# Attention evaluated in tile pairs: low parts of the odd tiles on VectorE, later padded values, value products in one step, query means and logarithms apart

## The chip, the cores and the metric

One core of one Trainium2 chip. The metric is the device time of one execution in microseconds (us), given as the median of three runs.

## The reference

A decoder trunk of two layers on an input of 1024 tokens by 1024 channels in float32. Layer 0 mixes tokens by a short gated convolution, layer 1 by sliding-window attention with sixteen query heads, four key/value heads and a window of 128; each mixer is followed by a SwiGLU feed-forward part. The change lies in layer 1's mixer, of which this is the core:

```
q = rmsnorm(q, q_gain); k = rmsnorm(k, k_gain)        # per head, 64 wide
scores = einsum('bnqkgd,bnskd->bnkgqs', qb, kw) * scale
scores = scores + alibi;  scores = where(mask, scores, -inf)
p = softmax(concat([scores, sink_col], -1))[..., :-1]
out = einsum('bnkgqs,bnskd->bnqkgd', p, vw)
out = out.reshape(bsz, s, N_Q_HEADS * HEAD_DIM) @ w_o
```

## The kernel before, in words

**Split operands.** All large products are made in float32 precision from two rounded operands: a high part (a copy rounded by ScalarE or VectorE) and a low part (what the rounding left out, by a subtraction). A product is three matmuls: high by high, high by low, low by high.

**Tiles, pairs and units.** The sixteen heads lie in eight tiles of 128 channels (two heads each), numbered 0 to 7; tiles 2p and 2p+1 are pair p. The attention takes one tile and one block of 128 queries at a time, a unit `(tile, block)`. `units` (L2408) lists 64 of them, numbered n here: pair p has units 16p to 16p+15, block by block, the even tile at even n and the odd tile at odd n. So unit 1 is tile 1's first block, unit 17 that of tile 3, unit 33 of tile 5, unit 49 of tile 7.

**Steps and their order.** All engines execute their instructions in the order in which the program issues them, and this order is written by hand (`tc.manual_schedule`, L2547). `step` (L2426) issues one step of a software pipeline that has eight lead-in steps before unit 0; step n works on unit n and some before it. The string `ORDER` (L59) says what a step issues, a letter at a time:

- `S`: scores of unit n on TensorE (four matmuls, L2245 and L2246, into the one bank P0). `M`: VectorE adds the distance bias and takes the minima (L2260), which frees P0. `E`: ScalarE's exponentials of unit n-1 (L2280).
- `T`: TensorE turns unit n-2 (L2288) into bank P1 (odd tile) or P3 (even tile); `H` and `L`: its high part by ScalarE (L2323) and low part by VectorE (L2329). Whichever of P1 and P3 isn't being turned into is `pos["free"]`, and statistics and rows (below) use it.
- `V`: the value products of a pair of units (L2343). Sub-block 0 is issued at even n for the units n-4 and n-3, sub-block 1 at odd n for n-5 and n-4. Each is up to four matmuls of 256 columns into one bank. `O` (odd n) and `o` (even n): ScalarE copies half of the result out (L2358), VectorE adds the other half (L2360), and the bank is free.
- `D`: what is due of the softmax division: sums widened by GpSimd (L1803), turned by TensorE (L1808), multiplied in by VectorE (L2388).
- `P`: a piece of other TensorE work. Through unit 39 it is the projection of the next pairs' queries (`work_of_pairs`, L2517; matmuls L2004), three pieces a step with 21 matmuls in four steps; from unit 40 on the first half of the output projection (L171, L175).
- `k` and `K`: what has been planned for the half step and for the end of the step. `plan(d, f)` (L2413) puts f d steps ahead.

**A tile's queries.** When the projection of a tile is finished, `keep_q` (L2137) plans its normalisation over the next steps: squares by ScalarE (L2146); at 2.5 steps, in a `k`, statistics by TensorE (sixteen matmuls with two columns, L1678), the mean by VectorE (L1685) and the logarithm by ScalarE (L1697); at 3, in the `K`, ScalarE's exponential (L1702) and a Newton step in VectorE's four small instructions (L1704 to L1711); the result is widened by GpSimd (L1803), turned by TensorE (L1808) and multiplied in by VectorE (L1813); then, per half of the tokens and per head, a high part by ScalarE (L2176) and a low part by GpSimd (L2181, function `part_lo`). `later` shifts the whole plan by so many steps. With it go GpSimd's low parts of the weights (`split_granule`, L1948, after VectorE's high part L1947), which are loaded by the sync engine's queue (L1941), and streamed operands on the same queue (L2507).

**Padded values.** The value products need copies of the values with 64 of the 128 rows zeroed. `load_padded` (L2310) has GpSimd zero the room on its first call (L2307, L2308) and then issues two DMAs of 128 KB (L2316) on the sync engine's queue.

Of the kernel before, what the change touches and what calls it, by code (L numbers as in the profile page):

```python
# [12 lines left out]
AF = mybir.ActivationFunctionType  # L13
# [42 lines left out]
KEYS_AS_PAIR = 4  # L56
STREAMED = (5, 2, 3, 4)

ORDER = "SPTMEoDkPHLVOPK"  # L59


EARLY = 4
# [25 lines left out]
def trunk_kernel(ctx: ExitStack, tc: tile.TileContext, xT, small, w_in, w_out, w_q, w_v, w_o, w_gu, w_dn, out):  # L88
# [1571 lines left out]
    def attention_layer():  # L1660
# [36 lines left out]
            act.activation(y, m, AF.Ln)  # L1697
            return y

        def head_guess(y, inv):  # L1700

            act.activation(y, y, AF.Exp, scale=-0.5)  # L1702
            t = slot("hr_t", (P, NB, 2), bufs=2)
            dve.tensor_tensor(t, y, y, ALU.mult)  # L1704
            if inv is not None:
                dve.tensor_tensor(y, y, inv.unsqueeze(1).to_broadcast([P, NB, 2]), ALU.mult)
            return t
# [429 lines left out]
        def keep_q(i, raw_of, side=None, later=0, steps=False):  # L2137

            t = {}

            def squares(h):
                if "raw" not in t:
                    t["raw"] = raw_of()
                    wide = slot("X2" if i else q_tag(i, 1)) if side is None else side
                    t["side"] = [wide[:, h * 512 : h * 512 + 512] for h in (0, 1)]
                act.activation(t["side"][h], t["raw"][:, h * 512 : h * 512 + 512], AF.Square)  # L2146

            def stats_of(b0=0, n=NB):
                if "st" not in t:
                    t["st"] = bank(pos["free"])  # L2150
                for b in range(b0, b0 + n, 2):
                    head_stats(t["st"], t["side"][b // 4][:, b % 4 * P : (b % 4 + 2) * P], b, 2)

            def mean():
                t["m"] = head_mean(t["st"])
                t["y"] = head_log(t["m"])

            def guess():
                t["t"] = head_guess(t["y"], cst[:, C_INVS + 2 * i : C_INVS + 2 * i + 2])

            def newton():
                head_newton(t["y"], t["t"], t["m"])


            def halves(e):
                rows = [slice(0, HD), slice(HD, P)]
                return rows[e], rows[1 - e]

            def raw_half(h, rows):
                return t["raw"][rows, h * 512 : h * 512 + 512].rearrange("p (s q) -> p s q", q=SUB)  # L2170

            def part_hi(h, e):
                rows, _ = halves(e)
                if e == 0:
                    Q.setdefault(i, []).append(slot(q_tag(i, h), (P, 8, 2, SUB), F32R))
                act.copy(Q[i][h][rows, :, e, :], raw_half(h, rows))  # L2176

            def part_lo(h, e, eng=pool):
                rows, rest = halves(e)
                q = Q[i][h]  # L2180
                eng.tensor_tensor(q[rest, :, e, :], raw_half(h, rows), plain(q)[rows, :, e, :], ALU.subtract)  # L2181

            rows_of = lambda h: scale_rows(t["raw"], t["side"][h], h, bank(pos["free"]))
            wide_of = lambda h: spread(pool, t["side"][h], t["y"][:, 4 * h : 4 * h + 4, :])

            if steps:
                shared = lambda h: spread(act, t["side"][h], t["y"][:, 4 * h : 4 * h + 4, :])
                return SimpleNamespace(
                    squares1=lambda: squares(1),
                    squares0=lambda: squares(0),  # L2190
                    stats=stats_of,
                    mean=mean,
                    guess=guess,
                    newton=newton,
                    wide0=lambda: shared(0),
                    wide1=lambda: shared(1),
                    rows0=lambda: rows_of(0),
                    rows1=lambda: rows_of(1),
                    hi0=lambda: part_hi(0, 0),
                    hi1=lambda: part_hi(0, 1),  # L2200
                    hi2=lambda: part_hi(1, 0),
                    hi3=lambda: part_hi(1, 1),
                    lo0=lambda: part_lo(0, 0),
                    lo1=lambda: part_lo(0, 1, dve),
                    lo2=lambda: part_lo(1, 0),
                    lo3=lambda: part_lo(1, 1),
                )
            first, rows = 1, (4.5, 5.5)
            for d, fs in (
                (first, [lambda: squares(0)]),  # L2210
                (first + 0.5, [lambda: squares(1)]),
                (1.5 + first, [stats_of, mean]),
                (2 + first, [guess, newton]),
                (rows[0] - 1.5, [lambda: wide_of(0)]),
                (rows[0] - 0.5, [lambda: wide_of(1)]),
                (rows[0], [lambda: rows_of(0)]),
                (rows[0] + 0.5, [lambda: part_hi(0, 0)]),
                (rows[1], [lambda: rows_of(1), lambda: part_lo(0, 0)]),
                (rows[1] + 0.5, [lambda: part_hi(0, 1)]),
                (rows[1] + 1, [lambda: part_lo(0, 1)]),  # L2220
                (rows[1] + 1.5, [lambda: part_hi(1, 0)]),
                (rows[1] + 2, [lambda: part_lo(1, 0)]),
                (rows[1] + 2.5, [lambda: part_hi(1, 1)]),
                (rows[1] + 3, [lambda: part_lo(1, 1)]),
            ):
                for f in fs:
                    plan(d + later, f)
# [80 lines left out]
                pool.memset(plain(padded[p][1])[0:SUB], 0.0)  # L2308

        def load_padded(p, q):  # L2310
            if p not in padded:
                pad_rooms(p)
            for sub in (0, 1):
                rows = slice(sub * SUB, (sub + 1) * SUB)
                src = plain(v[q])[rows, :, p].rearrange("p b l d -> p b (l d)")
                nc.sync.dma_start(plain(padded[p][sub])[rows, 4 * q : 4 * q + 4], src)  # L2316
# [96 lines left out]
        def plan(d, f):  # L2413

            agenda.setdefault(pos["step"] + d, []).append(f)
# [10 lines left out]
        def step(work, full=True):  # L2426


            n = pos["n"]
            pos["n"] += full  # L2430
            at = lambda d, f: f(*units[n - d]) if full and 0 <= n - d < NU else None

            def value(d, sub):
                if full and 0 <= n - d < NU and (n - d) % 2 == 0:
                    i, b = units[n - d]
                    values(i // 2, b, sub)

            def rest(d, step_):
                if full and 0 <= n - d < NU and (n - d) % 2 == 0:
                    keep_o(*units[n - d], step_)  # L2440

            pos["piece"] = 0

            def piece():
                next(work, None)
                pos["piece"] += 1

            calls = {
                "S": lambda: at(0, scores),
                "T": lambda: at(2, turn),  # L2450
                "V": lambda: [value(4, 0), value(5, 1)],
                "O": lambda: rest(5, 0),
                "o": lambda: rest(6, 1),
                "M": lambda: at(0, maxima),
                "E": lambda: at(1, exponents),
                "D": lambda: [f() for f in due.pop(n, [])] if full else None,
                "H": lambda: at(2, turn_hi),
                "L": lambda: at(2, turn_lo),
                "P": piece,
                "k": planned_early,  # L2460
                "K": planned,
            }
            for c in ORDER:
                calls[c]()
# [52 lines left out]
        def work_of_pairs():  # L2517
            n = 0
            for j in range(n_first, len(seq)):
# [4 lines left out]
                for p in range(NK // 2):  # L2524
# [3 lines left out]
                    for i in range(3):  # L2528
                        next(steps)
                        n += 1  # L2530
                        if i == 2 and streamed:
                            after_use(used["n"])
                            used["n"] += 1
                        if i == 2 and p == NK // 2 - 1:
                            finish(u, k, soon)
                            if k == 1:
                                keep_q(2 * u, lambda u=u: raw_of_even(u))
                            if k == 4:
                                raw, side = raw_of_odd(u)
                                keep_q(2 * u + 1, lambda raw=raw: raw, side, later=2)  # L2540
                        if n % 7 in (2, 4, 5, 0):
                            yield
# [4 lines left out]
        with tc.manual_schedule(engines={E.PE, E.Activation, E.DVE, E.Pool, E.SP}):  # L2547
# [4 lines left out]
            for d, g, e in ((12, 0, 1), (28, 1, 0), (34, 1, 1)):  # L2552
                for i, dd in enumerate((0, 0.5, 1.5, 3.5)):
                    plan(d + dd, lambda g=g, e=e, i=i: it["part"](g, e, i))
            for d, p, q in ((1, 0, 0), (3, 0, 1), (18, 1, 0), (19, 1, 1), (38, 2, 0), (45, 2, 1), (52, 3, 0), (53, 3, 1)):
                plan(d, lambda p=p, q=q: load_padded(p, q))
            keep_q(1, lambda: rooms["odd"], later=0)
            work = work_of_pairs()
# [167 lines left out]
```

## Time and profile before

| what | value |
|---|---|
| median of 3 runs (lowest, highest) | 1961.82 us (1961.06, 1962.26) |
| the profiled execution, its time | 1957.65 us |
| its span, first to last instruction | 1955.8 us |
| TensorE busy, whole span | 1923.0 us (98%) |
| VectorE, ScalarE, GpSimd busy | 67%, 45%, 16% |
| TensorE's mean granted clock | 0.991 of full speed |

The profile's page shows the busy share of each engine over the span in 40 equal slices of 49 us, and the granted clock below them. The attention's pipeline fills slices 22 to 26 (about 1036 to 1276 us). A row of the time line is: start, length, engine, line, operation, what it writes and reads, how many instructions are merged in it, and in brackets how long the engine sat idle before it and which instruction's end released it. "SPq" is the sync engine's queue.

### The profile page before, as it was taken

The numbers are of one execution on the slowest core, as the hardware profiler recorded it, in microseconds if no ns is written. First come the engines' busy times: TensorE is split into PE (matmuls) and PEld (weight loads), VectorE is DVE, ScalarE is ACT, GpSimd is POOL, SyncE is SP. The second block draws the span as 40 slices with busy tenths as digits, with TensorE's granted clock in tenths as the row PEclk, the third lists the DMA queues.
The fourth block names the chain that finished last, engine by engine and source line by source line (L and its number), as shares of the span: only waits on it lengthen the run. The fifth ranks groups of instructions, "written<-read, shape, count | busy, mean of one in ns | idle before, by whom it ended". The sixth has DMA issues, their size and how long they took to land. (4 is left out here: it accounts for less than half of the span.)

```text
span 1955.8 us, 25343 instructions
## 1 busy us (share of the span) xinstructions
PE 1923.0 (98%) x8989; PEld 1602.0 (82%) x8989; DVE 1316.0 (67%) x2293; ACT 886.8 (45%) x1753; POOL 310.6 (16%) x394
## 2 busy tenths in 40 slices
PE   9999999999999999999998889899999999999999
PEld 8888888888888888888987778788888888888887
DVE  8898867966556666556856676688765656565543
ACT  5543555533333334444555676555333333344441
POOL 0001221021111100100025465210111111100000
PEclk9999999999999999999998899999999999999999
DMA  8897594478887639975556651251674666468562
GB/s 318 255 240 168 126 249 144 130 256 232 233 239 212 173 122 349 310 215 177 212 217 214 190 179 35 89 185 55 231 194 143 195 188 180 125 234 281 196 231 100
DMA packets 160991, 382.53 MB, mean 196 GB/s; under 512 B 15840, under 2 KB 31328, under 8 KB 160864
## 3 DMA queue, kind: packets, MB, share of 16 engines
q1 hardware_dynamic: 125472, 271.55, 41.0%
q0 software_dynamic: 35248, 109.33, 22.9%
q8 instruction: 71, 1.16, 0.2%
q14 instruction: 56, 0.46, 0.1%
q10 hardware_dynamic: 144, 0.03, 0.0%
HBM read 304.04 MB, written 152.57 MB: 233 GB/s over the span
## 5 line engine op out<-in xcount | busy, mean ns | idle before, releaser
L1004 PE MATMUL acc<-XS,G 128*128 128x512 f32 x926 | 360.4, 389 | 0.0
L1007 PE MATMUL acc<-XS,G 128*128 128x512 f32 x926 | 360.3, 389 | 0.0
L1005 PE MATMUL acc<-XS,G 128*128 128x512 f32 x926 | 360.2, 389 | 0.0
L1004 PE MATMUL P<-A,G 128*128 128x512 f32 x550 | 214.1, 389 | 0.0
L1007 PE MATMUL P<-A,G 128*128 128x512 f32 x550 | 214.0, 389 | 0.0
L1005 PE MATMUL P<-A,G 128*128 128x512 f32 x550 | 214.0, 389 | 0.0
L1004 PEld LDWEIGHTS acc<-XS,G 128*128 128x128 f32 x926 | 173.8, 188 | 36.1
L1007 PEld LDWEIGHTS acc<-XS,G 128*128 128x128 f32 x926 | 173.8, 188 | 36.1
L1005 PEld LDWEIGHTS acc<-XS,G 128*128 128x128 f32 x926 | 173.8, 188 | 36.1
L1004 PE MATMUL acc<-A,G 128*128 128x512 f32 x442 | 172.1, 389 | 0.0
L1007 PE MATMUL acc<-A,G 128*128 128x512 f32 x442 | 172.0, 389 | 0.0
L1005 PE MATMUL acc<-A,G 128*128 128x512 f32 x442 | 171.9, 389 | 0.0
L938 DVE TENSOR_TENSOR G<-WL,G 128x512 fp32r<-128x512 f32 x168 | 115.0, 685 | 73.4 <-ACT G L937 73.4
L938 DVE TENSOR_TENSOR G<-WR,G 128x512 fp32r<-128x512 f32 (+1 forms) x216 | 144.2, 668 | 29.6 <-ACT G L937 29.6
L937 ACT CAST G<-WR 128x512 fp32r<-128x512 f32 (+1 forms) x216 | 130.5, 605 | 64.5 <-PE acc L1007 26.8
L937 ACT CAST G<-WH 128x512 fp32r<-128x512 f32 (+1 forms) x174 | 104.6, 601 | 84.4 <-PE acc L1007 40.8
L938 DVE TENSOR_TENSOR G<-WH,G 128x512 fp32r<-128x512 f32 (+1 forms) x174 | 115.5, 664 | 21.5 <-ACT G L937 21.3
L1339 ACT ACTIVATE G<-G 128x512 f32<-128x512 f32 x88 | 55.8, 634 | 159.2 <-DVE G L1436 153.1
L1004 PEld LDWEIGHTS P<-A,G 128*128 128x128 f32 x550 | 103.2, 188 | 21.4
L1005 PEld LDWEIGHTS P<-A,G 128*128 128x128 f32 x550 | 103.2, 188 | 21.4
L1007 PEld LDWEIGHTS P<-A,G 128*128 128x128 f32 x550 | 103.2, 188 | 21.4
L901 POOL DMA_DIRECT2D s<-s x68 | 60.1, 893 | 353.1 <-DMA s<-s 173.2
(440 smaller groups left out, 3793.3 us busy)
## 6 DMA issues: line engine op xcount, KB each, us to landing
G<-h SPq DMA_DIRECT2D x70, 512.0 KB, 4.8
s<-in_w_dn SPq DMA_DIRECT2D x32, 704.0 KB, 8.2
h<-X POOLq DMA_DIRECT2D x44, 512.0 KB, 4.9
s<-s POOLq DMA_DIRECT2D x32, 704.0 KB, 7.3
WR<-s SPq DMA_DIRECT2D x79, 256.0 KB, 4.1
WR<-in_w_gu SPq DMA_DIRECT2D x36, 512.0 KB, 5.4
WH<-in_w_gu SPq DMA_DIRECT2D x36, 512.0 KB, 4.4
XS<-q_ops SPq DMA_DIRECT2D x36, 512.0 KB, 5.4
```

What stands on the lines that cost most here:

```text
L901: nc.gpsimd.dma_start(dst[to], dst[of], accum_op=ALU.add)
L937: lambda: act.copy(out_hi, raw),
L938: lambda: lo_eng.tensor_tensor(out_lo, raw, plain(out_hi), ALU.subtract),
L1004: pe.matmul(ps, w[:, 0, c], x[:, 0, :], start=start and e == 0, stop=False, skip_group_check=True)
L1005: pe.matmul(ps, w[:, 0, c], x[:, 1, :], start=False, stop=False, skip_group_check=True)
L1007: pe.matmul(ps, w[:, 1, c], x[:, 0, :], start=False, stop=last, skip_group_check=True)
L1339: state["silu"] = act.activation(x, x, AF.Silu)
```

## The change

Five things, all in the attention's schedule:

- `ORDER` gets a letter `v`: both sub-blocks of the value products are issued at odd n for the units n-5 and n-4, sub-block 0 early in the step (after the first `P`), sub-block 1 where `V` stands. At even n there is none.
- The statistics' plan: the logarithm and exponential move to the end of the step that has the statistics, behind `H` and `O`; VectorE's small instructions and GpSimd's first widening move to the middle of the next step.
- The even tiles 2, 4 and 6 start their plan one step later (`later=1`), so that their statistics are issued at n = 7, 23 and 39 and no longer at 6, 22 and 38. The odd tiles keep their steps (12, 28 and 44).
- For odd tiles the low parts of the first half of the tokens (two subtractions a tile) go to VectorE.
- Zeroing the padded rooms is planned by itself, at steps 4, 17, 37 and 51 after the pipeline's begin (before: inside the loads, at 1, 18 and 52); the first pair's loads are at 7 and 9 (before: 1 and 3).

```
-ORDER = "SPTMEoDkPHLVOPK"
+ORDER = "SPvTMEoDkPHLVOPK"
...
+        def head_exp(y):
             act.activation(y, y, AF.Exp, scale=-0.5)
+
+        def head_guess(y, inv, exp=True):
+
+            if exp:
+                head_exp(y)
             t = slot("hr_t", (P, NB, 2), bufs=2)
...
+            def mean_only():
+                t["m"] = head_mean(t["st"])
+
+            def log():
+                t["y"] = head_log(t["m"])
+
             def mean():
-                t["m"] = head_mean(t["st"])
-                t["y"] = head_log(t["m"])
-
-            def guess():
-                t["t"] = head_guess(t["y"], cst[:, C_INVS + 2 * i : C_INVS + 2 * i + 2])
+                mean_only()
+                log()
+
+            def guess(exp=True):
+                t["t"] = head_guess(t["y"], cst[:, C_INVS + 2 * i : C_INVS + 2 * i + 2], exp)
...
+            low = dve if i % 2 else pool
             for d, fs in (
                 (first, [lambda: squares(0)]),
                 (first + 0.5, [lambda: squares(1)]),
-                (1.5 + first, [stats_of, mean]),
-                (2 + first, [guess, newton]),
-                (rows[0] - 1.5, [lambda: wide_of(0)]),
+                (1.5 + first, [stats_of, mean_only]),
+                (2 + first, [log, lambda: head_exp(t["y"])]),
+                (2.5 + first, [lambda: guess(False), newton, lambda: wide_of(0)]),
                 (rows[0] - 0.5, [lambda: wide_of(1)]),
                 (rows[0], [lambda: rows_of(0)]),
                 (rows[0] + 0.5, [lambda: part_hi(0, 0)]),
-                (rows[1], [lambda: rows_of(1), lambda: part_lo(0, 0)]),
+                (rows[1], [lambda: rows_of(1), lambda: part_lo(0, 0, low)]),
                 (rows[1] + 0.5, [lambda: part_hi(0, 1)]),
-                (rows[1] + 1, [lambda: part_lo(0, 1)]),
+                (rows[1] + 1, [lambda: part_lo(0, 1, low)]),
...
         def load_padded(p, q):
-            if p not in padded:
-                pad_rooms(p)
...
-                "V": lambda: [value(4, 0), value(5, 1)],
+                "v": lambda: value(5, 0),
+                "V": lambda: value(5, 1),
...
                             if k == 1:
-                                keep_q(2 * u, lambda u=u: raw_of_even(u))
+                                keep_q(2 * u, lambda u=u: raw_of_even(u), later=1)
...
-            for d, p, q in ((1, 0, 0), (3, 0, 1), (18, 1, 0), (19, 1, 1), (38, 2, 0), (45, 2, 1), (52, 3, 0), (53, 3, 1)):
+            for d, p in ((4, 0), (17, 1), (37, 2), (51, 3)):
+                plan(d, lambda p=p: pad_rooms(p))
+            for d, p, q in ((7, 0, 0), (9, 0, 1), (18, 1, 0), (19, 1, 1), (38, 2, 0), (45, 2, 1), (52, 3, 0), (53, 3, 1)):
                 plan(d, lambda p=p, q=q: load_padded(p, q))
```

More of the change, by code (lines that the diff above doesn't have):

```diff
@@ L1698, in head_log @@
             return y
-        def head_guess(y, inv):
+        def head_exp(y):
             act.activation(y, y, AF.Exp, scale=-0.5)
+        def head_guess(y, inv, exp=True):
+            if exp:
+                head_exp(y)
             t = slot("hr_t", (P, NB, 2), bufs=2)
```

## The prediction

> **What bounds the kernel now.** I read the page first, then the busy time by stage, then TensorE's groups in the attention with what ended their idle time, then the time line around the longest gaps. The page says that TensorE is the bound, and where it isn't whole:
>
> ```profile
> PE 1923.0 (98%) x8989; PEld 1602.0 (82%) x8989; DVE 1316.0 (67%) x2293; ACT 886.8 (45%) x1753; POOL 310.6 (16%) x394
> PEclk9999999999999999999998899999999999999999
> ```
>
> ```profile
> 1036.00:1190.00 154.00, 135.00 (x813) 117.98 (x812) 107.18 (x330) 102.23 (x316) 81.25 (x80) 0.90 0.54 171
> 1190.00:1276.00 86.00, 78.25 (x477) 65.10 (x477) 59.29 (x170) 54.28 (x174) 32.31 (x43) 1.00 0.21 69
> 1276.00:1955.00 679.00, 675.77 (x2994) 558.96 (x2994) 420.63 (x646) 263.18 (x446) 57.45 (x88) 1.00 0.57 182
> ```
>
> The columns are the stretch, its length, busy time of TensorE, its weight loads, VectorE, ScalarE and GpSimd, the granted clock, the DMA share. TensorE idles 32.8 us of the 1955.8 us span, and 19.0 + 7.75 of these lie in the attention. From 1276 us on it is busy 675.77 of 679.00: what the attention saves the end keeps. What the 26.75 us wait for:
>
> ```profile
> L2245 PE MATMUL P<-A,G 128*128 128x192 f32 (+2 forms) x128 | 32.7, 279 | 11.4 <-POOL G L2181 9.7 <-DVE mx L2260 1.8
> L1678 PE MATMUL P<-cst,X 128*128 128x2 f32 x80 | 10.7, 264 | 8.3 <-DVE G L2388 6.9 <-DVE X L2329 1.3
> L2343 PE MATMUL P<-G,A 128*128 128x256 f32 x58 | 15.1, 305 | 4.9 <-DVE XS L2360 2.9 <-ACT WH L143 1.8 <-ACT s L2280 0.3
> L2343 PE MATMUL P<-X,A 128*128 128x256 f32 x40 | 11.1, 307 | 1.3 <-ACT G L2280 0.7 <-ACT G L2323 0.4 <-DVE A L2360 0.2
> L2343 PE MATMUL P<-G,G 128*128 128x256 f32 x38 | 8.5, 287 | 0.4 <-DVE A L2360 0.4
> ```
>
> Scores wait 11.4 us, 9.7 of it for GpSimd's low parts; statistics 8.3; value products 4.9 + 1.3 + 0.4 = 6.6. Together 26.3, and each is one of the change's targets. Behind most long gaps TensorE also runs at half clock. These are the stretches of the attention in which the clock's row is 0.50:
>
> ```profile
> 1040.52:1047.35 6.83, 4.85 (x15) 4.10 (x16) 2.00 (x7) 1.05 (x6) 5.66 (x5) 0.50 0.11 38
> 1078.07:1081.48 3.41, 3.41 (x14) 3.12 (x14) 1.65 (x8) 2.05 (x8) 2.27 (x3) 0.50 1.03 305
> 1095.14:1098.55 3.41, 3.41 (x13) 2.86 (x12) 2.18 (x7) 0.63 (x2) 0.86 (x2) 0.50 0.00 0
> 1115.62:1119.03 3.41, 3.41 (x13) 3.02 (x14) 1.25 (x6) 1.57 (x7) 0.96 (x2) 0.50 0.00 2
> 1136.10:1142.92 6.82, 6.82 (x27) 6.04 (x27) 4.95 (x13) 2.89 (x12) 5.82 (x6) 0.50 0.49 145
> 1173.64:1180.47 6.83, 6.83 (x26) 6.04 (x26) 2.13 (x10) 2.47 (x9) 2.40 (x3) 0.50 0.01 4
> ```
>
> They hold 28.73 us of busy TensorE; at full clock that work takes half, so they cost 14.4 us. A single one costs 1.7. At most 26.75 + 14.4 = 41 us could go.
>
> **The change part by part.** Times are of the profiled execution (span 1955.8, its own time 1957.65); it lies 4.2 us below the median of 1961.82, and I take the saving from the median.
>
> *Unit 1's scores.*
>
> ```profile
> 1030.52 2.28 SPq L2316 DMA_DIRECT2D A<-A  x2
> 1033.55 0.56 SPq L1941 DMA_DIRECT2D WR<-in_w_q  x1
> ```
>
> ```profile
> 1039.19 0.43 DVE L1947 CAST WL<-WR 128x512 fp32r<-128x512 f32 x1 [3.33 <-DMA WR<-in_w_q]
> 1039.79 0.41 DVE L2260 CUSTOM_DVE_ANT_0 s<-P,cst 128x128 f32<-128x128 f32 x1
> 1041.19 2.60 POOL L2181 TENSOR_TENSOR G<-WH,G 64x512 fp32r<-64x512 f32 x2
> 1042.50 0.42 PE L2245 MATMUL P<-A,G 128*128 128x64 f32 x1 [3.67 <-POOL G L2181]
> ```
>
> ```profile
> L2181 DVE TENSOR_TENSOR G<-G,G x1: 777/777/777, 1024.5 to 1024.5; 64x512 fp32r<-64x512 f32 x1
> ```
>
> The padded loads hold the sync queue 2.28 us ahead of a weight load, for which VectorE then waits 3.33 us; GpSimd's low parts (1.3 us each) stand behind GpSimd's part of the same weights. Moved to steps 7 and 9, the padded loads let the weights go between 0 and 2.28 us earlier; an operand load between them still waits for TensorE, so I take 1.3. The low part on VectorE costs 0.78 us and stands before unit 0's minima, whose end (1040.20) frees P0. So unit 1's scores start at 1040.20 + 0.78 - 1.3 = 1039.7 instead of 1042.50: 2.8 us. With 0.9 us of idle left the half clock behind it goes too: 4.85 / 2 = 2.4. Sum **5.2**; bounds 1.5 (weights no earlier, half clock stays) and 3.67 + 2.4 = 6.1.
>
> *Units 6 to 12.* The statistics of tile 2 move off a step in which VectorE also adds a half result, and ScalarE's logarithm no longer stands ahead of `H`, so low parts and minima come sooner.
>
> ```profile
> 1075.03 0.36 PE L2245 MATMUL P<-A,G 128*128 128x192 f32 x1 [0.61 <-DVE mx L2260]
> 1076.38 1.86 PE L1678 MATMUL P<-cst,X 128*128 128x2 f32 x16
> ```
>
> The 1.8 us of scores waiting for minima lie here, and so does the half clock at 1078.07, which follows a gap of only 0.61 and 1.86 us of statistics. VectorE remains nearly as loaded, so I take half of both: **1.8** (0.9 + 0.85); bounds 0 and 3.5.
>
> *Units 17 and 22, then 33 and 38.*
>
> ```profile
> 1091.47 0.69 DVE L2388 TENSOR_TENSOR G<-G,P 128x512 f32<-128x512 f32 x1
> 1093.18 2.60 POOL L2181 TENSOR_TENSOR G<-WH,G 64x512 fp32r<-64x512 f32 x2
> 1094.50 0.30 PE L2245 MATMUL P<-A,G 128*128 128x64 f32 x1 [2.23 <-POOL G L2181]
> ...
> 1102.90 0.63 PE L2343 MATMUL acc<-X,A 128*128 128x256 f32 x4
> ...
> 1103.38 0.63 PE L2004 MATMUL acc<-XS,WL 128*128 128x512 f32 x2
> ...
> 1111.75 0.47 DVE L2260 CUSTOM_DVE_ANT_0 G<-P,cst 128x192 f32<-128x192 f32 x1
> 1113.14 0.69 DVE L2388 TENSOR_TENSOR G<-G,P 128x512 f32<-128x512 f32 x1
> 1113.88 2.03 PE L1678 MATMUL P<-cst,X 128*128 128x2 f32 x16 [3.43 <-DVE G L2388]
> ...
> 1154.52 0.30 PE L2245 MATMUL P<-A,G 128*128 128x64 f32 x1 [2.26 <-POOL G L2181]
> ...
> 1172.44 2.50 PE L1678 MATMUL P<-cst,X 128*128 128x2 f32 x16 [3.51 <-DVE G L2388]
> ```
>
> Unit 17 waits for GpSimd's low part. On VectorE two of these (0.78 each) join a queue with little slack: the division's multiply, ending at 1092.16, moves to about 1092.7, the second low part ends at 1093.5, and the scores start 0.95 us sooner. But TensorE arrives 0.5 us sooner as well (1102.90 to 1103.38), since four value products no longer stand at the end of unit 16's step. The gap shrinks from 2.23 to 1.8 only: the wait on GpSimd becomes one on VectorE, behind which minima and half results queue. At unit 22 the statistics needed the bank that the division's rows had just filled, so they waited for L2388. A step later they take the other bank. From 1110.45 on TensorE goes on with two pieces (0.5 us each, an estimate from the same rows), waits 0.8 for minima that end at 1112.2, does scores, a piece and four value products (1.5), and meets the same L2388 at its end (1113.83), since that frees the bank for the turn; the statistics then wait for the low part behind it, about as long as the multiply (0.69). So 3.43 becomes about 1.6. Of the half clock I count the stretch at 1095.14 as gone (1.7) and the one at 1115.62 as staying, since 1.6 of idle and 2.0 of statistics are more than what led to 1078.07. Sum 0.4 + 1.8 + 1.7 = **3.9**; bounds 0.4 and 9.1 (all idle and both stretches). The next pair has the same places with 2.26 and 3.51, and I expect one of its two half-clock periods at 1173.64 to go: **3.9** again.
>
> *Odd tiles' statistics, unit 49.*
>
> ```profile
> 1134.71 2.35 PE L1678 MATMUL P<-cst,X 128*128 128x2 f32 x16 [1.03 <-DVE X L2329]
> 1212.51 0.30 PE L2245 MATMUL P<-A,G 128*128 128x64 f32 x1 [1.48 <-POOL G L2181]
> ```
>
> Tile 5's statistics stay where they are, with their low part and the 6.82 us of half clock behind: **0**, between -1 (tile 4's rows now come later in VectorE's queue) and +4.4. Unit 49 is as unit 17: **0.5**, between 0 and 1.5.
>
> *Value products.* From 1190 us on all have one bank, P2.
>
> ```profile
> 1236.64 0.87 DVE L2360 TENSOR_TENSOR XS<-P,XS 64x256 f32<-64x256 f32 x2
> 1237.66 0.47 PE L2343 MATMUL P<-G,A 128*128 128x256 f32 x2 [1.04 <-ACT WH L143]
> ```
>
> Sub-block 0 stands at the end of the very step in whose middle VectorE frees the bank (1237.51); the label of the releaser is a later ScalarE end, the time fits L2360. After the change scores and a piece of the next step come first, about 1.0 us of work by the rows at 1102.90, so 1.04 is almost covered. Eleven such gaps make the 6.6; I leave 1.5: **5.1**, bounds 3 and 6.6. In the first stage the banks alternate and the move costs nothing but the shift counted above.
>
> *Subtractions on VectorE beside GpSimd.*
>
> ```profile
> L1704 DVE TENSOR_TENSOR hr_t<-hr_y x10: 165/176/997, 994.5 to 1198.1; 128x16 f32<-128x16 f32 x10
> ```
>
> The same small instruction takes 165 to 997 ns, so VectorE is sometimes held for 0.8 us. If all of the eight moved low parts were held so, VectorE would lose 6.6 us; few stand on the path: **-1.0**, bounds -5 and 0. [...]
>
> The new zeroing steps and the first widening only change their place in GpSimd's queue (81.25 busy of 154.00); the widening of tiles 3 and 5 now stands behind the even tile's last low part, at most 1.3 us, of which the step in between covers all but a little. Zero, and up to 1.3 for each of two.
>
> Sum: 5.2 + 1.8 + 3.9 + 3.9 + 0 + 0.5 + 5.1 - 1.0 = **19.4 us**; 1961.82 - 19.4 = **1942.4 us**. With some terms near their bounds this case lies between 1934 and 1950.
>
> **Rivals.** *VectorE takes the place of each wait in the first stage.* An even step now gives TensorE no value product while VectorE has minima, two half results, often a multiply; the low parts add eight times 0.78. Against it: 107.18 us busy of 154.00. Then only the first unit and the value products pay: 5.2 + 5.1 - 1.0 = 9.3, 1952.5 us.
>
> *The clock heals as a whole.* If only a gap of about a stretch's own length (3.4 us) halves the clock, no gap left does: the idle terms give 2.8 + 0.9 + 2.2 + 2.2 + 0.5 + 5.1 - 1.0 = 12.7, the clock all of 14.4, together 27.1: 1934.7 us. Against it stands 1078.07 after 0.61 of idle. [...]
>
> *Slower: the clock stays low.* TensorE's work is now uneven, light at even n, and it must wait for VectorE there. If in many even steps idle plus tiny matmuls pass about 2.4 us in 3.4 (the sum that led to 1078.07), the clock halves again and again at 1.7 us each. Of the 240 us from 1036 to 1276, 70 such stretches, a third would cost 39 us: 1942.4 + 39 = 1981 us. It decides from twelve stretches on (19.4 / 1.7). Against it: gaps of 1.0 to 1.5 us (1212.51, 1237.66) stand ahead of no stretch at 0.50.
>
> *It changes nothing:* the waits only move, within 3 us of 1961.8.
>
> **How the numbers follow.** My forecast 0.64, VectorE 0.15, whole clock 0.12, slower 0.05, nothing 0.04. A measurement of this kernel can tell about 0.2% (3.9 us) from no change. Faster has the first three: 0.91; same 0.04; slower 0.05. The range runs from 1931 (beyond the whole clock's value) to 1955 (beyond VectorE's); it leaves out the last two cases and the tails of the others, under 0.2.
>
> **What would show it.** Right: no scores waiting for L2181 on GpSimd; unit 1's scores under 1 us of idle; no statistics waiting for L2388; L2343's idle time under 2 us; fewer stretches at 0.50. TensorE's idle from 1036 on falls from 26.75 to about 13, and what is left is put down to VectorE (minima, L2329, L2181). Wrong: gaps at units 17 and 33 as long as before, rows (L1808) waiting for GpSimd's L1803, or a clock's row under 0.90 in the first stage.

## The result, and the profile after

| | before | after |
|---|---|---|
| median (lowest, highest) of 4 runs | 1961.65 us (1961.06, 1962.26) | 1933.23 us (1930.83, 1934.18) |
| profiled execution, its time and span | 1957.65, 1955.8 us | 1933.44, 1931.6 us |
| TensorE's mean granted clock | 0.991 | 0.997 |

The ratio is 0.9853 with a 95% interval of 0.9836 to 0.987: the change saves 28.4 us, where the forecast was 19.4. The time lies inside the range, 9 us below the predicted one. First the page: engine totals, and the clock's row over the 40 slices.

```profile
PE 1912.5 (99%) x8989; PEld 1595.9 (83%) x8989; DVE 1324.1 (69%) x2301; ACT 887.5 (46%) x1753; POOL 302.0 (16%) x386
PEclk9999999999999999999999999999999999999999
```

The same 8989 matmuls keep TensorE busy 10.5 us less (1923.0 before). The clock accounts for it: the dip in the attention's slices is gone, and the stretches at half clock (0.50) take 10.2 us in place of 34.1 (the six of the prediction and one at 1030.28); half of that difference, 12 us, is a little more than these 10.5. The other 13.7 us of the span's 24.2 are idle time. By stage (stretch, length, busy time of TensorE, its weight loads, VectorE, ScalarE, GpSimd, clock, DMA):

```profile
1036.00:1190.00 154.00, 143.72 (x920) 125.68 (x919) 125.25 (x374) 114.47 (x352) 85.92 (x86) 0.97 0.56 176
1190.00:1250.00 60.00, 58.65 (x368) 51.22 (x367) 47.65 (x133) 42.38 (x138) 20.65 (x29) 1.00 0.25 86
```

In the attention 10.28 + 1.35 = 11.6 us of idle are left of 26.75; the forecast was about 13. The clock's mean in the first stage rises from 0.90 to 0.97. The groups of TensorE in the attention that still wait, and the value products:

```profile
L2008 PE MATMUL acc<-XS,WL 128*128 128x512 f32 x208 | 69.4, 425 | 1.1 <-DMA XS<-q_ops 1.1
L2256 PE MATMUL P<-A,G 128*128 128x192 f32 (+2 forms) x128 | 31.6, 271 | 7.3 <-DVE G L2191 4.6 <-DVE mx L2271 2.7
L2352 PE MATMUL P<-G,A 128*128 128x256 f32 x58 | 14.4, 294 | 0.0
L1678 PE MATMUL P<-cst,X 128*128 128x2 f32 x96 | 11.7, 251 | 1.1 <-DVE X L2338 0.9 <-ACT X L2150 0.2
L1812 PE MATMUL P<-cst,X 128*128 128x128 f32 x48 | 7.6, 280 | 3.7 <-POOL X L1807 3.7
```

Lines have moved by some ten: scores are L2256, low parts L2191, minima L2271, value products L2352, the division's multiply L2397, widening L1807, rows L1812. The value products' waits (6.6) are all gone, and so is the statistics' wait for the multiply (6.9). Scores wait for VectorE's low parts (4.6) instead of GpSimd's (9.7), for minima somewhat more than before (2.7 for 1.8), and two waits are new: rows for GpSimd's widening, 3.7, and streamed operands, 1.1. Most of the longer gaps on TensorE's time line:

```profile
1053.74 0.36 PE L2256 MATMUL P<-A,G 128*128 128x192 f32 x1 [0.98 <-DVE mx L2271]
...
1087.67 0.30 PE L2256 MATMUL P<-A,G 128*128 128x64 f32 x1 [1.71 <-DVE G L2191]
1106.07 0.36 PE L2256 MATMUL P<-A,G 128*128 128x192 f32 x1 [1.04 <-DVE mx L2271]
...
1124.74 1.95 PE L1678 MATMUL P<-cst,X 128*128 128x2 f32 x16 [0.85 <-DVE X L2338]
1134.07 0.66 PE L1812 MATMUL P<-cst,X 128*128 128x128 f32 x4 [0.87 <-POOL X L1807]
1142.93 0.30 PE L2256 MATMUL P<-A,G 128*128 128x64 f32 x1 [1.59 <-DVE G L2191]
...
1195.95 0.30 PE L2256 MATMUL P<-A,G 128*128 128x64 f32 x1 [1.35 <-DVE G L2191]
```

These are minima in an early step (1053.74), unit 17 (1087.67), the minima ahead of the even tile's new statistics (1106.07), tile 5's statistics and rows, unit 33, unit 49. The stretches whose clock is 0.50:

```profile
1089.25:1092.66 3.41, 3.41 (x15) 3.03 (x13) 1.31 (x3) 1.44 (x4) 1.07 (x1) 0.50 0.00 0
1126.79:1130.21 3.42, 3.42 (x13) 2.94 (x13) 3.42 (x8) 2.37 (x8) 3.35 (x2) 0.50 0.49 155
1143.86:1147.27 3.41, 3.41 (x16) 3.11 (x15) 1.95 (x7) 0.48 (x1) 0.16 (x1) 0.50 0.00 0
```

10.2 us are left, one stretch behind each of three gaps above. Unit 1, the largest single term of the forecast:

```profile
1031.63 1.15 SPq L1945 DMA_DIRECT2D WR<-in_w_q  x1
1036.76 1.32 SPq L2325 DMA_DIRECT2D A<-A  x2
1037.51 0.43 DVE L1951 CAST WL<-WR 128x512 fp32r<-128x512 f32 x1 [0.25 <-DMA WR<-in_w_q]
1037.97 0.69 DVE L2191 TENSOR_TENSOR G<-WH,G 64x512 fp32r<-64x512 f32 x1
1039.52 0.27 PE L2256 MATMUL P<-A,G 128*128 128x64 f32 x1
```

The weight load now stands ahead of the padded loads in the sync queue, VectorE waits 0.25 us for it instead of 3.33, and the scores start at 1039.52 (forecast 1039.7) with no gap in front.

### The profile page after: what moved, and what is told of

Same layout as the page of the kernel before. It is cut to its first block, busy times and chain, and to the rows that moved or that the text cites. A ratio compares the mean times of both kernels' runs of the same rounds, so it can differ in the third digit from the quotient of the medians.

```text
span 1931.6 us, 25337 instructions
## 1 busy us (share of the span) xinstructions
PE 1912.5 (99%) x8989; PEld 1595.9 (83%) x8989; DVE 1324.1 (69%) x2301; ACT 887.5 (46%) x1753; POOL 302.0 (16%) x386
## 4 chain that ended last, share of the span: by engine, by line
PE 94%; DVE 3%; ACT 2%; issue 1%; DMA 0%; POOL 0%; DVEq 0%; POOLq 0%; ACTq 0%
PE acc L1007 16%; PE acc L1005 16%; PE acc L1004 16%; PE P L1004 10%; PE P L1007 10%; PE P L1005 10%; PE acc L171 3%; PE P L2008 2%; PE acc L2008 1%; PE acc L175 1%; PE P L2352 1%; PE acc L1137 1%; PE P L1678 1%; PE acc L1139 1%; PE acc L1138 1%
```

## The experiments

Five kernels undo one part of the change each.

**The value products.** `ORDER` and the calls as before:

```
-ORDER = "SPvTMEoDkPHLVOPK"
+ORDER = "SPTMEoDkPHLVOPK"
...
-                "v": lambda: value(5, 0),
-                "V": lambda: value(5, 1),
+                "V": lambda: [value(4, 0), value(5, 1)],
```

> The changed kernel with the value products as before (sub-block 0 at the end of the even step). Part-by-part theory: the second stage gets its waits of the value products back, 5 to 6.6 us of TensorE idle, and nothing else moves: about 1939 us. Rival (the uneven steps cost something in the first stage): the odd tiles' first scores, which wait 1.71 and 1.59 us in the changed kernel, wait about 0.5 less because TensorE arrives later, and their half clock goes too, so that only 1 to 3 us are lost: about 1935 us.

1941.61 us (1939.66 to 1943.96), ratio to before 0.9908 (0.9894 to 0.9923): 8.4 us lost of the 28.4. From its time line and its groups on TensorE:

```profile
1088.06 0.30 PE L2256 MATMUL P<-A,G 128*128 128x64 f32 x1 [1.23 <-DVE G L2191]
```

```profile
1234.17 0.47 PE L2352 MATMUL P<-G,A 128*128 128x256 f32 x2 [1.03 <-DVE XS L2369]
```

```profile
L2352 PE MATMUL P<-G,A 128*128 128x256 f32 x58 | 14.2, 291 | 5.0 <-DVE XS L2369 2.9 <-ACT WH L143 1.8 <-ACT s L2291 0.3
L2352 PE MATMUL P<-X,A 128*128 128x256 f32 x40 | 10.2, 287 | 0.9 <-DVE A L2369 0.5 <-ACT G L2332 0.4
L2352 PE MATMUL P<-G,G 128*128 128x256 f32 x38 | 8.3, 283 | 0.4 <-DVE A L2369 0.4
```

The waits come back, 6.3 us of them, at 1.0 us where VectorE frees the one bank in the middle of the step (1234.17). For the odd tiles' first scores in the first stage the old order is better by half a microsecond a pair (unit 17 waits 1.23, not 1.71; unit 33 1.12, not 1.59), since TensorE arrives later. So the move pays in the second stage and costs a little in the first. The mean clock of the four runs is 0.995 to 0.997 (0.996 to 0.998 with the whole change), and both traces have 10.2 us at half clock, so this part hardly works through the clock. Of the 8.3 us between the two profiled spans 5.0 are idle time; the same matmuls are also busy for 3.3 us longer, which no run here explains.

The same part alone, on the kernel before (the first two lines of that edit the other way round, and the calls with them):

> The kernel before with the value products' move alone. Part-by-part theory: the second stage's eleven waits (6.6 us) go and the rest stays: 6 to 8 us under the kernel before, about 1954 us. Rival (with uneven steps TensorE reaches the odd tiles' first scores sooner, and waits for GpSimd's low part as much longer): their gaps of 2.23, 2.26 and 1.48 us grow by about 0.5 each, more half clock follows, and only 2 to 5 us remain.

1953.87 us (1950.51 to 1954.77) against 1960.87 beside it, ratio 0.9964 (0.9951 to 0.9976): 7.0 us. Its value products have 0.0 us of idle in every group; what remains of the first stage's waits is longer:

```profile
1094.00 0.42 PE L2245 MATMUL P<-A,G 128*128 128x64 f32 x1 [2.72 <-POOL G L2181]
1115.23 3.58 PE L1678 MATMUL P<-cst,X 128*128 128x2 f32 x16 [3.45 <-DVE G L2388]
```

Unit 17 waits 2.72 where it waited 2.23: the predicted earlier arrival of 0.5 us, seen by itself.

**The low parts.** All on GpSimd again:

```
-            low = dve if i % 2 else pool
+            low = pool
```

> The changed kernel with all low parts on GpSimd. Part-by-part theory: unit 1's scores wait 1 to 2.5 us again, units 17, 33 and 49 about 0.5 more each than in the changed kernel, and one or two more stretches of half clock follow: 4 to 7 us, about 1938 us. Rival (VectorE is the bound in the first stage, and the moved subtractions cost there what they save): within 2 us of 1933.

1937.13 us (1936.29 to 1939.99), ratio 0.9888 (0.9873 to 0.9902): 3.9 us lost.

```profile
1040.85 0.30 PE L2256 MATMUL P<-A,G 128*128 128x64 f32 x1 [1.45 <-POOL G L2191]
...
1090.99 0.30 PE L2256 MATMUL P<-A,G 128*128 128x64 f32 x1 [2.61 <-POOL G L2191]
...
1147.11 0.42 PE L2256 MATMUL P<-A,G 128*128 128x64 f32 x1 [2.44 <-POOL G L2191]
```

Each odd tile's first scores wait some 0.9 us more than with the change, and unit 1's 1.45 more. That is what VectorE's faster subtraction (0.69 us for GpSimd's 1.3) is worth in this place.

**The even tiles' later statistics.** Back at their old step:

```
-                                keep_q(2 * u, lambda u=u: raw_of_even(u), later=1)
+                                keep_q(2 * u, lambda u=u: raw_of_even(u))
```

> The changed kernel with the even tiles' plan at its old step. Part-by-part theory: the statistics of tiles 4 and 6 wait for the division's multiply again, 3.4 us each in place of about 1, and one more stretch of half clock each: 6 to 8 us, about 1940 us. Rival (the shift only moves the work and crowds GpSimd, whose widening makes TensorE's rows wait 3.7 us in the changed kernel): no change or 1 to 2 us faster.

1942.09 us (1941.16 to 1942.3), ratio 0.9909 (0.9893 to 0.9926): 8.9 us lost, with the value products the largest of the five. Its time line, and the clock behind:

```profile
1107.74 3.58 PE L1678 MATMUL P<-cst,X 128*128 128x2 f32 x16 [3.42 <-DVE G L2397]
```

```profile
1106.50:1116.70 10.20, 8.96 (x35) 8.28 (x36) 3.19 (x13) 1.54 (x7) 3.49 (x4) 0.50 0.44 150
1167.90:1174.70 6.80, 6.80 (x27) 6.22 (x28) 2.04 (x10) 1.83 (x7) 0.64 (x2) 0.50 0.03 12
```

The statistics again wait for the division's multiply (3.42, and 3.50 in the next pair). With them the clock is down for 10.2 and 6.8 us, and all its runs have a mean of 0.993 where the change has 0.997: over 1940 us these 0.004 are 7.8 us. Of the 8.7 us between the two profiled spans 6.1 are longer busy time. So most of what this part is worth comes through the clock.

**The logarithm's place.** Logarithm, exponential, small instructions and the first widening at their old places:

```
-                (1.5 + first, [stats_of, mean_only]),
-                (2 + first, [log, lambda: head_exp(t["y"])]),
-                (2.5 + first, [lambda: guess(False), newton, lambda: wide_of(0)]),
+                (1.5 + first, [stats_of, mean]),
+                (2 + first, [guess, newton]),
+                (rows[0] - 1.5, [lambda: wide_of(0)]),
```

> The changed kernel with logarithm, exponential and Newton step at their old places. Part-by-part theory: ScalarE's high parts stand behind the logarithm again (1 to 2 us), but the rows no longer wait for GpSimd's widening (3.7 us): within 2 us of 1933. Rival (the logarithm ahead of the high part held VectorE's low part, and so the next minima, in every tile): 4 to 6 us slower, about 1938 us, with scores waiting for minima for 1.5 us and more.

1933.04 us (1931.23 to 1935.37), ratio 0.9865 (0.985 to 0.988): no difference in time. The rows' waits for GpSimd vanish for tiles 2 to 7 (1.5 us are left of 3.7), and waits for minima take their place, 6.1 us for 2.7, this being the longest:

```profile
1133.68 0.36 PE L2256 MATMUL P<-A,G 128*128 128x192 f32 x1 [1.40 <-DVE mx L2271]
```

The new places free VectorE's and ScalarE's queues in one half step and delay GpSimd's widening in another. The two don't quite cancel: the profiled execution has 2.9 us more idle time than the changed kernel's and 0.9 us less busy time, with one stretch at half clock in place of three. So the equal medians may owe something to the clock, and a worth of up to 3 us isn't ruled out.

**The padded loads.** The first pair's back at steps 1 and 3, with each pair's zeroing inside its first load:

```
         def load_padded(p, q):
+            if p not in padded:
+                pad_rooms(p)
...
-            for d, p in ((4, 0), (17, 1), (37, 2), (51, 3)):
-                plan(d, lambda p=p: pad_rooms(p))
-            for d, p, q in ((7, 0, 0), (9, 0, 1), (18, 1, 0),
+            for d, p, q in ((1, 0, 0), (3, 0, 1), (18, 1, 0),
...
```

> The changed kernel with the padded values loaded at the old steps. Part-by-part theory: the weights for which VectorE waits at 1037.5 us land 1.3 us later, unit 1's scores start as much later: 1 to 2 us, up to 4 with a stretch of half clock, about 1935 us. Rival (the load was never in the way, TensorE's use of the operand rooms is): no change, within 1 us of 1933.

1936.16 us (1935.37 to 1936.71), ratio 0.9889 (0.9867 to 0.991): 2.9 us lost.

```profile
1030.53 1.30 SPq L2327 DMA_DIRECT2D A<-A  x2
1032.62 1.13 SPq L1945 DMA_DIRECT2D WR<-in_w_q  x1
1039.26 0.43 DVE L1951 CAST WL<-WR 128x512 fp32r<-128x512 f32 x1 [2.68 <-DMA WR<-in_w_q]
1039.72 0.69 DVE L2191 TENSOR_TENSOR G<-WH,G 64x512 fp32r<-64x512 f32 x1
```

```profile
1041.27 0.39 PE L2256 MATMUL P<-A,G 128*128 128x64 f32 x1 [2.46 <-ACT s L2291]
```

The weight load stands behind the padded ones and is issued 1 us later; VectorE waits 2.68 us for it, and the low part behind it ends at 1040.41. Unit 1's scores wait 2.46 (the releaser named is a later end by ScalarE).

The five losses, 8.4 + 3.9 + 8.9 + 2.9 and a gain of 0.2, make 23.9 of the 28.4 us. The changed kernel was not run again beside these five. By the ratios to the kernel before, whose median beside them was 1960.97 or 1959.25 us, the losses are 10.8, 6.9, 11.0, 2.4 and 7.1 us, 38 together. So each loss is sure to 2 to 4 us only, and whether the parts add up to the whole stays open.

**What holds the clock.** The statistics' matmuls (two columns each) are issued a second time into the same bank, for seven tiles. The results stay as they are; TensorE has only more tiny work.

```
-                (1.5 + first, [stats_of, mean_only]),
+                (1.5 + first, [stats_of, stats_of, mean_only]),
```

> The changed kernel with every tile's sixteen statistics matmuls issued twice in a row into the same places: seven tiles, 1.9 us each, 13 us of tiny matmuls more and no wait added. If matmuls of two columns keep the clock as idle time does not, the time grows by 13 us less what their length hides (VectorE catches up behind them): 8 to 13 us, 1941 to 1946 us. If they count as idle for the clock, 3.8 us of them in a stretch of 3.4 halve the clock after nearly each tile, at 1.7 to 3.4 us: another 8 to 14 us, 1950 to 1958 us, and the clock's row shows 6 to 9 stretches at 0.50 in place of 3.

1957.19 us (1956.07 to 1958.47), ratio 0.9995 (0.9985 to 1.0004): 24 us slower than the changed kernel, nearly as much as the whole change, as expected for the case that such matmuls count as idle. Its idle time is 2.8 us less (span 1954.5 less 1938.2 busy). The clock is halved in eight stretches of 40.8 us together. Two of them, then what stands ahead of the second:

```profile
1139.10:1145.90 6.80, 6.80 (x29) 6.32 (x28) 2.31 (x8) 2.48 (x8) 5.95 (x4) 0.50 0.26 92
...
1200.60:1207.40 6.80, 6.80 (x27) 6.22 (x27) 3.24 (x12) 1.72 (x7) 3.04 (x4) 0.50 0.00 0
```

```profile
1197.57 0.49 PE L2299 MATMUL P<-cst,s 128*128 128x128 f32 x3
1197.89 4.38 PE L1678 MATMUL P<-cst,XS 128*128 128x2 f32 x32
1202.13 1.20 PE L171 MATMUL acc<-A,WH 128*128 128x512 f32 x2
```

No gap at all: TensorE is issuing without pause from before 1197 on, and the clock falls at 1200.6, after 2.7 of the 4.38 us of two-column matmuls. Of the 22.9 us between the two profiled spans up to (40.8 - 10.2) / 2 = 15.3 are the clock, the other 7.6 or more the added work less the idle time that it fills.

**Towards a better version.** Where unit 17 still waits for VectorE, the low part runs beside GpSimd's. From the time line of the changed kernel:

```profile
1083.23 0.69 DVE L2191 TENSOR_TENSOR G<-WH,G 64x512 fp32r<-64x512 f32 x1
...
1086.75 0.87 DVE L2191 TENSOR_TENSOR G<-WH,G 64x512 fp32r<-64x512 f32 x1
1087.25 1.52 POOL L2191 TENSOR_TENSOR G<-WH,G 64x512 fp32r<-64x512 f32 x1 [0.17 <-ACT G L2186]
```

The second low part is planned half a step behind its high part, and that is when TensorE already waits. `e_lo` puts both high parts into one half step and the second low part of odd tiles half a step sooner:

```
-                (rows[0] + 0.5, [lambda: part_hi(0, 0)]),
+                (rows[0] + 0.5, [lambda: part_hi(0, 0), lambda: part_hi(0, 1)]),
                 (rows[1], [lambda: rows_of(1), lambda: part_lo(0, 0, low)]),
-                (rows[1] + 0.5, [lambda: part_hi(0, 1)]),
-                (rows[1] + 1, [lambda: part_lo(0, 1, low)]),
+                (rows[1] + (0.5 if i % 2 else 1), [lambda: part_lo(0, 1, low)]),
```

> The changed kernel with the odd tiles' second low part on VectorE half a step sooner (its high part on ScalarE with it), so that it stands ahead of the next unit's minima, half results and the division's multiply. Theory (the first scores of units 17, 33 and 49 wait 1.71, 1.59 and 1.35 us for this place in the queue only): 3 to 4 of these 4.65 us go, and two half-clock stretches with 1.7 each: 5 to 7 us, about 1927 us. Rival (VectorE is bound there): the wait moves to the minima of the next units, 0 to 2 us.

1927.04 us (1926.4 to 1927.45), ratio 0.9842 (0.9824 to 0.986): 6.2 us below the changed kernel's median and, with the next one, the fastest of all. The runs of the two don't overlap (the slowest here 1927.45, the fastest there 1930.83), though the intervals of their ratios do. Of the 7.1 us between the profiled spans 4.2 are idle time. Its time line at unit 17:

```profile
1082.47 0.69 DVE L2191 TENSOR_TENSOR G<-WH,G 64x512 fp32r<-64x512 f32 x1
...
1084.13 0.69 DVE L2191 TENSOR_TENSOR G<-WH,G 64x512 fp32r<-64x512 f32 x1
...
1085.59 0.30 PE L2255 MATMUL P<-A,G 128*128 128x64 f32 x1
```

No low part is waited for any more (4.6 us gone), and one stretch of half clock is left. `e_lo_pool` is the same with `low = pool`:

> The version with the second low part half a step sooner, but with all low parts on GpSimd again. Theory (what counts is the place in the queue, ahead of the next step's division work, not the engine): units 17, 33 and 49 wait under 0.5 us, unit 1 waits 1.45 us as in the version with the low parts on GpSimd, so 1928 to 1930 us. Rival (GpSimd's 1.3 us a piece are too long there): these units wait 1 to 2 us, 1933 us and more.

1927.52 us (1926.86 to 1928.51), ratio 0.9832 (0.9819 to 0.9846): the same time.

```profile
1082.93 2.63 POOL L2191 TENSOR_TENSOR G<-WH,G 64x512 fp32r<-64x512 f32 x2
...
1085.79 0.19 PE L2255 MATMUL P<-A,G 128*128 128x64 f32 x1
```

GpSimd needs twice as long (2.63 us for two, VectorE 0.69 for one), ends at 1085.56, and the scores start with no gap. Unit 1, for which a wait of 1.45 us was expected, waits 0.60, and for minima. So the engine mattered only while the subtraction stood in the wrong place of the queue.

Two more steps on `e_lo`. `e_both` also delays the even tiles' last low part by a step (and the first zeroing), so that the rows don't wait for GpSimd; `e_split` computes the odd tiles' statistics in two halves, a step apart (`half_stats(h)` issues eight of the sixteen matmuls and the mean of that half).

```
-                (rows[1] + 3, [lambda: part_lo(1, 1)]),
+                (rows[1] + (3 if i % 2 else 4), [lambda: part_lo(1, 1)]),
...
-            for d, p in ((4, 0), (17, 1), (37, 2), (51, 3)):
+            for d, p in ((5, 0), (17, 1), (37, 2), (51, 3)):
```

```
-                (1.5 + first, [stats_of, mean_only]),
+                (0.5 + first, [lambda: half_stats(0)] if i % 2 else []),
+                (1.5 + first, [lambda: half_stats(1)] if i % 2 else [stats_of, mean_only]),
```

> As the one before, and the even tiles' last low part on GpSimd a step later, the first zeroing a step later, so that neither stands ahead of an odd tile's widening. Theory: the rows' 3.7 us of waiting for the widening fall to about 1: 2 to 3 us less than the one before, about 1925 us. Rival (the widening waits for VectorE's Newton step anyway): no difference from the one before.

> The version with the second low part half a step sooner, and the odd tiles' statistics in two halves of eight matmuls, one step apart, each with its own bank and mean. Theory of the clock (tiny matmuls count as idle, so 1.9 us of them behind a wait of 0.86 halve it): no half clock at tile 5's statistics, and their wait of 0.86 is halved: 1 to 2.5 us under 1927.0. [...]

1928.25 us (1926.07 to 1929.21) and 1929.5 us (1928.36 to 1931.73): neither gains on `e_lo`. In `e_both` the rows' wait for GpSimd falls from 3.5 to 1.0 us, as expected, but the division's rows now wait 1.0 for VectorE, 0.2 in `e_lo`. Idle time in the attention (1036 to 1250) is 6.7 us, 0.9 less than in `e_lo`, while its profiled execution has 10.2 us of half clock for 3.4. In `e_split` the first half's matmuls wait for the squares instead, and half clock follows them all the same: behind them the scores' matmuls from 1125.73 to 1126.56 last 0.41 us each, the same ones from 1128.99 on 0.27 to 0.28. The matmuls that wait:

```profile
1122.33 1.09 PE L1678 MATMUL P<-cst,X 128*128 128x2 f32 x8 [1.16 <-ACT X L2150]
```

## Why the prediction was right, and where it was off

**Idle time: the sum was right, its terms less so.** The terms without their clock parts were 19.4 - 6.65 = 12.75 us; the two profiled executions differ by 13.7. By places: unit 1 starts at 1039.52 (1039.7 said). Units 17 and 33 wait 1.71 and 1.59 (1.8 said, as a wait for VectorE). Ahead of the even tile's statistics minima cost 1.04 (0.8 said), but the statistics themselves don't wait, where 0.7 more was expected. Tile 5's wait of 1.03 is 0.85. Unit 49 gains 0.13 and not 0.5. In units 6 to 12 the waits for minima fall from 1.76 to 0.98 (half of them said), and the stretch at 1078.07 is gone (half of it counted). That the sum fits so well is in part luck: the value products gave 1.5 us more than said and the even tiles' statistics 1.4, while rows waiting for GpSimd and streamed operands took 4.8 that were put at nothing.

**Value products: 5.1 said, 6.6 gone** in the trace, 7.0 as measured alone. The step that left 1.5 us was too cautious.

**VectorE beside GpSimd: -1.0 said.** The moved low parts feel it little: one takes 0.69 us by itself, 0.87 at 1086.75 and at most 1.03 (unit 49) beside GpSimd's, which takes 1.52 instead of about 1.3. The longer holds are of other instructions, like this cast, which took 0.43 us in unit 1's rows:

```profile
1126.75 2.38 POOL L1888 TENSOR_TENSOR A<-X,A 64x1024 fp32r<-64x1024 f32 x1
1127.28 2.13 DVE L1951 CAST WL<-WR 128x512 fp32r<-128x512 f32 x1
```

From 1015 to 1265 us VectorE's instructions last 8.6 us longer in sum than is usual for their line and shape (the lower quartile; differences above 0.1 us counted), against 4.9 in the kernel before. With all low parts on GpSimd again it is 8.2. So the change as a whole does add 3.7 us of holds, not far from the bound of -5, but hardly any by the moved low parts, and their move is worth +3.9 by its undoing.

**New places in GpSimd's queue: zero said, 3.7 us of waits.** Rows waiting for GpSimd's L1803 were named as a sign of error, and they came. Tile 5's wait of 0.87 is the one that the prediction feared, behind the even tile's last low part, and 0.75 in the lead-in stand behind the zeroing. In the four others (0.68, 0.32, 0.69, 0.35) GpSimd is free, and the widening starts 0.13 to 0.17 us after VectorE's Newton step ends, which the change put half a step later; that term was left out. Undoing that part moves the waits and not the time.

**The clock is the term that was mis-sized**, and it is where most of the 9 us lie. I counted 6.65 us: some stretches as gone, 1115.62 as staying, tile 5's as untouched. In the profiled executions 10.5 went, and not just the ones that I counted. Unit 1's is gone as said. All of the even tiles' stretches are gone, 1115.62 with them, tile 5's 6.82 is 3.42, and one at 1030.28, ahead of the pipeline, is gone that no term had. Against that unit 17's, which I counted as gone, is still there (1089.25), and unit 33 has a new one (1143.86). And the profiled execution of before was a good one. The prediction took the 4.2 us between it and the median to be nothing of the change's business. Yet four runs of before, each with its mean clock, are 1953.42 us at 0.993, 1957.03 at 0.992, 1959.38 at 0.990 and 1962.12 at 0.989: from first to last 8.7 us, of which 0.004 of 1958 us are 7.8. Runs of before at its median have 0.989, so they lose another 0.002 x 1958 = 3.9 us to the clock against the traced one (an estimate from clocks rounded to 0.001, so good to 2 us); the changed kernel's four runs stay at 0.996 to 0.998. So 1.0 us of the miss is idle time, 3.9 the stretches of the trace, and the remaining 4.2 by this estimate those that the median run has and the trace hasn't.

**The rivals.** The time is nearest to the whole clock's 1934.7, but its mechanism didn't hold: three stretches follow gaps of 1.71, 0.85 (with 1.95 of statistics) and 1.59. VectorE didn't take the place of each wait (1952.5): its share of the scores' waits is 4.6 + 2.7 us. The slower case needed twelve stretches; there are three. Its mechanism, the clock falling behind tiny matmuls, showed in the run with doubled statistics: 40.8 us at half clock in place of 10.2, with 2.8 us less idle time.

## What to carry to other kernels

When an engine waits for another's result, look first for the half step in which the result is queued: with the low part half a step sooner, GpSimd's slow subtraction did as well as VectorE's fast one (1927.52 and 1927.04 us). Count two-column matmuls as gaps when you price the clock (issued twice, they took half clock from 10.2 to 40.8 us here), and keep them apart from other waits. Before taking a saving from one trace to the median, compare the two runs' mean clock: here it was 0.991 in the trace and 0.989 at the median, by the estimate above 3.9 us that the trace doesn't show.

## What the runs showed of the hardware

- Behind two-column matmuls issued back to back TensorE's clock fell to 0.50 with no idle time ahead: at 1200.6 in the run with doubled statistics, after 2.7 us of them.
- The stretches at 0.50 listed from the traces of before and after last 3.41 to 3.42 or 6.82 to 6.83 us.
- The length of a gap didn't decide by itself whether half clock came within it or just behind. In the kernel before it came with gaps of 3.67 (ahead of 1042.50), 2.23 (1094.50), 3.43 (1113.88) and 3.51 us (1172.44), with 1.03 ahead of 2.35 us of statistics (1134.71), and behind 0.61 (1075.03) and 1.86 us of statistics; it didn't come with 2.26 (1154.52), 1.48 (1212.51) or 1.04 (1237.66). In the changed kernel it came with 1.71 (1087.67), 1.59 (1142.93) and 0.85 ahead of 1.95 us of statistics (1124.74), and not with 1.35 (1195.95), 1.04 (1106.07) or 0.98 (1053.74); nor did it with 1.70 at unit 17 with the old logarithm (1090.43), where the matmuls behind keep their 0.28 us. What else decides stays open.
